# Four intermediate arrays of the first token block kept in the recurrence's on-chip buffers

## The chip, the cores and the metric

The kernel runs on one core of one Trainium2 chip. The metric is the device time of one execution in microseconds (us), lowest possible. All tensors are float32; the large matrix products split each operand into a rounded high part and a low rest, and take three matmuls for one product.

## The reference, cut to what matters

One inference step of a small trunk for 1024 prompt tokens and 8 x 16 sample tokens, width 1024, 16 heads of 64. Layer 0 is an RWKV-7 time mixing with a SwiGLU feed-forward part, layer 1 an attention in bands with another feed-forward part. The change lies in the time mixing of layer 0:

```python
r = xr @ w_r
w_log = -softplus(-(w0 + tanh(xw @ w1) @ w2)) - 0.5
decay = exp(-exp(w_log))
k = xk @ w_k
v = xv @ w_v
a_gate = sigmoid(a0 + (xa @ a1) @ a2)
g = sigmoid(xg @ g1) @ g2
kk = l2_normalize(heads(k * k_k))
k = k * (1.0 + (a_gate - 1.0) * k_a)
y, state = wkv7_scan(r, decay, k, v, -kk, kk * a_gate, state0)
...
bonus = sum_per_head(r * k * r_k) * v
out = ((groupnorm(y) + bonus) * g) @ w_o
```

Here `xr`, `xw`, ... are six mixes of each token's normed input with that of the token before it.

## The kernel before, in words

The 1152 tokens are three blocks b = 0, 1, 2 of 384 (`NB`, `TB`). For each block `proj(b)` computes the projections, feature tile by feature tile: f = 0 to 7, a tile being 128 features x 384 tokens. Its parts run in this order:

- `proj_lora`: the small products with w1, a1 and g1, then `second("w2", ..., "cs")` and `second("a2", ..., "a")`. For each f they put two matmuls into a PSUM bank of the tag `acc` (two banks), take a sigmoid on ScalarE (ACT, line 548) and, for the decay, a running sum along the tokens on VectorE (DVE, line 550). The results are the decay sums **cs** and the rates **a**. After that the gate g is evicted (line 596) and spilled.
- `proj_k`: for each f, 24 matmuls with `rw_k` into an `acc` bank. From cs two exponentials (lines 649 and 651), from a the factor of the key (line 658), from the bank a square (line 654), its sum over each head by one more matmul into the bank `aux`, a reciprocal root (lines 660 to 662) and six products on DVE (lines 663 to 674). Line 665 is the last that reads the bank. One result is the modified key **kp**. Three others are spilled to DRAM for the recurrence.
- `proj_r`: the same 24 matmuls with `rw_r`; with cs (line 514) and kp (line 515) it makes the scaled r and, by one more matmul, the **bonus** factor bn (line 521).
- `proj_v`: with `rw_v`; it multiplies v by bn (line 614).

The four arrays cs, a, kp and bn pass from one part to the next through DRAM: `save` (line 501) writes a tile of 192 KB to `sf`, `load` (line 498) brings it back. Per f that is four writes and five reads (cs is read by `proj_k` and again by `proj_r`), all issued by SyncE (SP).

Beside the projections runs the recurrence, in windows of 128 tokens, w = 0 to 8, each in two halves of the heads. `inverses(b)` inverts the small triangular matrices of the block's three windows beside `proj_r(b)` and the parts behind it: `win_first` multiplies (bank `G`), the result goes through DRAM (`ld`, `L`), a loop of 30 short DVE instructions solves it (lines 814 and 815), it goes through DRAM again (`Z`, `TT`), and `win_merge` joins the pieces by DVE transposes (`t`, line 835) and small matmuls (bank `st`). The windows of block b run beside `proj(b + 1)`; those of the last block run beside the output projection `outproj` of the blocks before. They load their inputs from DRAM into the buffers of the tags `XL`, `BKT`, `UV` and `YL`, three of each. In block 0 no window runs yet. Until the first windows these buffers serve only as landing place for a few weights of the adaLN modulation at the start (`self.early`).

A scheduler puts the instructions of each engine in order, guided by a timeline of its own; each engine then works through its list strictly in order and waits at an instruction whose input is not there. So the order on PE, DVE, ACT and SP can change at places that the source does not touch. DMAs of these parts are issued by SP, those of the inverses partly by ACT; both queues, too, work in order.

The lines before that the steps below touch: 473 (`spill`), 498 and 501, 514 to 521, 548 and 550, 583 (the load of the table set for logarithm and exponential), 614, 649 to 674.

Of the kernel before, what the change touches and what calls it, by code (L numbers as in the profile page):

```python
# [10 lines left out]
AF = mybir.ActivationFunctionType  # L11
# [6 lines left out]
TB = 384  # L18
KF = 8
KAPPA = float(np.exp(-0.5))  # L20
# [116 lines left out]
def mm(nc, out, lhsT, rhs, start, stop):  # L137
    return nc.tensor.matmul(out, lhsT, rhs, start=start, stop=stop)  # L138


class Trunk:
# [110 lines left out]
    def split(self, hi, lo, x):  # L252
        self.nc.scalar.activation(hi, x, AF.Copy)  # L253
        self.nc.vector.tensor_tensor(lo, x, hi, ALU.subtract)  # L254
# [220 lines left out]
    def proj(self, b):  # L475

        if b == 0:
            self.lw = {}
            ring = (f() for _ in range(2) for f in self.early)
            self.ada = self.ada_steps((0, 2, 1, 3), "acc", 2, lambda: next(ring))  # L480
            self.A0 = [self.cp.tile([128, 9], F32, name=f"A0_{f}") for f in range(8)]
            self.proj_h(0)
            self.x = self.hsplit()
            self.ada = self.ada_steps(range(4, 12))
        x, k = self.x, self.mixed(2, b)
        yield from self.proj_lora(b, *x)
        r = self.mixed(0, b)
        yield from self.proj_k(b, *k)
        v = self.mixed(3, b)
        yield from self.alternate(self.inverses(b), self.proj_r(b, *r))  # L490
        if b + 1 < NB:
            self.proj_h(b + 1)
        yield from self.proj_v(b, *v)
        if b + 1 < NB:
            self.x = self.hsplit()

    def load(self, t, n, b, f):
        self.nc.sync.dma_start(t, self.sf[b][n][:, f])

    def save(self, n, b, f, t):  # L500
        self.nc.sync.dma_start(self.sf[b][n][:, f], t)

    def proj_r(self, b, hi, lo):

        nc = self.nc
        for f in range(8):
            W = self.wunit(self.pp, self.a["rw_r"][f])
            pz = self.bank("acc", 2)
            self.gemm(pz[:, :TB], W, hi, lo)
            kp = self.ev("ag", 2)  # L510
            self.load(kp, "kp", b, f)
            ex = self.ev("rr", 2)
            self.load(ex, "cs", b, f)
            nc.scalar.activation(ex, ex, AF.Exp, scale=-KAPPA)
            nc.vector.scalar_tensor_tensor(kp, pz[:, :TB], self.P("rk", f), kp, ALU.mult, ALU.mult)
            nc.vector.tensor_tensor(ex, ex, pz[:, :TB], ALU.mult)
            self.spill("r", b, f, ex)
            aux = self.bank("aux", 1)
            mm(nc, aux[:, :TB], self.C("bo"), kp, True, True)
            bn = self.ev("e0", 3)  # L520
            nc.scalar.activation(bn, aux[:, :TB], AF.Copy)
            self.save("bn", b, f, bn)
            yield

    def proj_lora(self, b, hi, lo):

        nc, pp = self.nc, self.pp
        split = lambda ts: tuple([self.hgroups(t)[i] for t in ts] for i in range(2))
        (hc, hp), (lc, lp) = split(hi), split(lo)

        def first(n, rows):
            pw = self.bank("acc", 2)
            W = self.lora_in(n)
            for i, (h, l) in enumerate(((hc, lc), (hp, lp))):
                for k in range(8):
                    s = slice(k * rows, (k + 1) * rows)
                    self.mm3(pw[:rows, :TB], W[i][0][:, s], W[i][1][:, s], h[k], l[k], i + k == 0, i + k == 8)
            return pw

        def second(n, t, bias, spill):  # L540
            wh, wl = self.wunit(pp, self.a[n])
            for f in range(8):
                fs = slice(f * 128, (f + 1) * 128)
                pz = self.bank("acc", 2)
                mm(nc, pz[:, :TB], wh[:, fs], t, True, False)
                mm(nc, pz[:, :TB], wl[0:64, fs], t[0:64], False, True)
                sg = self.ev("e0", 3)
                ins = nc.scalar.activation(sg, pz[:, :TB], AF.Sigmoid, bias=self.P(bias, f))
                if spill == "cs":
                    nc.vector.tensor_tensor_scan(sg, rs, sg, 0.0, ALU.mult, ALU.add)  # L550
                self.save(spill, b, f, sg)
                if f % 4 == 3:
                    yield
            self.last_sg = ins

        pw = first("wa1", 128)
        yield
        tw, ta = self.ev("ag", 2, F32R), self.ev("ag", 2, F32R)
        th = self.ev("kp")
        nc.scalar.activation(th[:64], pw[:64, :TB], AF.Tanh)  # L560
        self.split(tw[0:64], tw[64:128], th[:64])
        th = self.ev("kp")
        nc.scalar.activation(th[:64], pw[64:128, :TB], AF.Copy)
        self.split(ta[0:64], ta[64:128], th[:64])
        pg = first("g1a", 128)
        yield
        th = self.ev("kp")
        h, l = self.ev("rr", 2, F32R), self.ev("rr", 2, F32R)
        nc.scalar.activation(th, pg[:, :TB], AF.Sigmoid)
        self.split(h, l, th)  # L570
        pg = first("g1b", 32)
        yield
        th = self.ev("kp")
        t = self.ev("vv", 2, F32R)
        nc.scalar.activation(th[:32], pg[:32, :TB], AF.Sigmoid)
        self.split(t[0:32], t[32:64], th[:32])
        nc.scalar.activation(t[64:96], th[:32], AF.Copy)
        rs = self.ev("rs", 1)
        nc.sync.dma_start(rs, self.a["rs"][b // 2])
        yield from second("w2", tw, "w0", "cs")  # L580
        yield from second("a2", ta, "a0", "a")
        with self.tc.issue_after(self.last_sg.ins):
            nc.scalar.preload_act_table_set("natural_log_exp_and_others")
        ah, al = self.wunit(pp, self.a["g2a"])
        raw = pp.tile([128, 1024], F32, tag="raw", name=self.nm("raw"), bufs=self.nraw)
        nc.sync.dma_start(raw[:96], self.a["g2b"])
        bh = pp.tile([128, 1024], F32R, tag="whi", name=self.nm("whi"), bufs=self.nhi)
        nc.scalar.activation(bh[:96], raw[:96], AF.Copy)
        nc.vector.tensor_tensor(bh[64:96], raw[64:96], bh[64:96], ALU.subtract)
        for f in range(8):  # L590
            fs = slice(f * 128, (f + 1) * 128)
            pz = self.bank("acc", 2)
            self.mm3(pz[:, :TB], ah[:, fs], al[:, fs], h, l, True, False)
            mm(nc, pz[:, :TB], bh[:96, fs], t[:96], False, True)
            g = self.ev("e0", 3)
            nc.scalar.activation(g, pz[:, :TB], AF.Copy)
            self.spill("g", b, f, g)
            if f % 4 == 3:
                yield

    def proj_v(self, b, hi, lo):

        nc = self.nc
        for f in range(8):
# [2 lines left out]
            self.gemm(pz[:, :TB], W, hi, lo)  # L607
            if b in (2,):
                self.step(1)
            vv = self.ev("vv", 2)  # L610
            self.load(vv, "bn", b, f)
            v = self.ev("e0", 3)
            nc.scalar.activation(v, pz[:, :TB], AF.Copy)
            nc.vector.tensor_tensor(vv, vv, pz[:, :TB], ALU.mult)
# [18 lines left out]
    def proj_k(self, b, hi, lo):  # L633

        nc = self.nc
        self.eend = self.eends[b]
        for f in range(8):
            W = self.wunit(self.pp, self.a["rw_k"][f])
            pz = self.bank("acc", 2)
            self.gemm(pz[:, :TB], W, hi, lo)  # L640
            iv = self.ev("rr", 2)
            self.load(iv, "cs", b, f)
            ag = self.ev("ag", 2)
            self.load(ag, "a", b, f)
            ext = self.pp.tile([128, 408], F32, tag="ext", name=self.nm("ext"), bufs=1)
            for s, sx, n, i in self.spans(b):
                ev = ext[:, sx].rearrange("p (g t) -> p g t", t=n + 1)
                nc.gpsimd.memset(ev[:, :, 0:1], 1.0)
                nc.scalar.activation(ev[:, :, 1:], iv[:, s].rearrange("p (g t) -> p g t", t=n), AF.Exp, scale=-KAPPA)
                nc.gpsimd.tensor_copy(self.eend[:, f, i:i + ev.shape[1]], ev[:, :, n])  # L650
            nc.scalar.activation(iv, iv, AF.Exp, scale=KAPPA)
            sq = self.ev("sq", self.nsq)
            kk = self.ev("kk")
            nc.scalar.activation(sq, pz[:, :TB], AF.Square, scale=self.P("kk", f))
            aux = self.bank("aux", 1)
            mm(nc, aux[:, :TB], self.C("bo"), sq, True, True)
            kp = self.ev("kp")
            nc.scalar.activation(kp, ag, AF.Identity, bias=self.oka[:, f:f + 1], scale=self.P("ka", f))
            inv = self.ev("inv", self.nsq)
            nc.vector.tensor_scalar(inv, aux[:, :TB], 1e-24, None, ALU.max)  # L660
# [1229 lines left out]
```

## Time and profile before

| | |
|---|---|
| median of 3 runs | 3863.73 us (3863.69 to 3864.73) |
| span of the profiled execution, first to last instruction | 3893.4 us |
| mean granted TensorE clock over that span | 0.927 |
| TensorE (PE) matmuls busy | 3557.4 us, 91% |
| DVE busy | 2281.8 us, 59% |
| ACT busy | 1578.1 us, 41% |
| moved by DMA | 551.91 MB |

The profile gives the span of one execution and no other time of it; this span is 29.7 us longer than the median of the runs that were timed without a profile. Block 0 covers, in this profile, about 88 us (first sigmoid of the decay) to 320 us (last tile of `proj_v`): `second` and the gate to 130 us, `proj_k` to 195, `proj_r` to 250, `proj_v` to 320. The four stages are named A, B, C and D below.

Rows of a wait view read "engine, what it writes, line <- what ended the wait: us in total, times, longest". Rows of a timeline read "start, duration, engine, line, operation, out<-in, shapes, count [idle before it <- what ended that]"; with a count above 1 they merge neighbours. A row of a stretch gives for each engine the busy us and the count of instructions, then the granted TensorE clock (PEclk, 1 is full), the share of time in which the DMA engines were busy, and GB/s.

### The profile page before, as it was taken

Reading aid. Unit: us, or ns where it says so; the run is one execution under the profiler, and the core shown is the slowest. Engines: PE = TensorE matmul, PEld = TensorE weight load, DVE = VectorE, ACT = ScalarE, POOL = GpSimd, SP = SyncE. Lnnn points to the kernel's source line nnn. Section 1 sums busy time; section 2 is a strip of 40 time slices with the busy share of each in tenths; the row PEclk is TensorE's granted clock in tenths of the full one; section 3 lists DMA queues with packets and bytes.
Section 4 is the critical chain, followed back from the end, with each engine's and each line's share of the span. In section 5 each row is a group of like instructions: output and inputs, shape, how many; then the busy total and the mean of one; then the engine's idle time right before and its main releaser. Section 6 shows DMA issues by size and latency. Waiting matters only on the chain.

```text
span 3893.4 us, 72370 instructions
## 1 busy us (share of the span) xinstructions
PE 3557.4 (91%) x28662; PEld 3135.3 (81%) x28662; DVE 2281.8 (59%) x4355; ACT 1578.1 (41%) x2987; POOL 571.8 (15%) x473
## 2 busy tenths in 40 slices
PE   6789988988889789999999899888889899999999
PEld 4677777777667689999888789777777789999998
DVE  4567566666435775555456842576675765454567
ACT  4554545554213443333411253465654533333310
POOL 0000000000000154454000100000000264454000
PEclk8887988789768989999999999999999899999999
DMA  5775776577646522222655213355464422222521
GB/s 195 223 223 150 202 231 164 143 225 201 179 127 191 177 92 74 76 73 76 235 202 203 83 53 101 108 158 156 147 192 155 138 74 76 74 74 94 169 82 72
DMA packets 429347, 551.91 MB, mean 142 GB/s; under 512 B 128432, under 2 KB 297520, under 8 KB 424528
## 3 DMA queue, kind: packets, MB, share of 16 engines
q1 hardware_dynamic: 374864, 528.41, 42.9%
q10 hardware_dynamic: 54144, 18.89, 2.2%
q8 instruction: 225, 3.69, 0.4%
q14 instruction: 114, 0.93, 0.1%
HBM read 413.03 MB, written 134.12 MB: 141 GB/s over the span
## 4 chain that ended last, share of the span: by engine, by line
PE 62%; DMA 7%; DVE 6%; ACT 3%; issue 2%; SPq 1%; POOL 0%; ACTq 0%; DVEq 0%; POOLq 0%
PE S L138 31%; PE PT L138 15%; PE acc L138 7%; PE st L138 2%; PE O L138 2%; DVE h L254 1%; PE PT L1716 1%; PE G L138 1%; PE Y L138 1%; PE aux L138 1%; ACT pts L1717 1%; DMA h<-qT 0%; DMA h<-in_wq 0%; DVE wlo L254 0%; DVE x L325 0%
## 5 line engine op out<-in xcount | busy, mean ns | idle before, releaser
L138 PE MATMUL S<-h,w 128*128 128x320 f32 (+1 forms) x4944 | 697.6, 300 | 19.8 <-DVE h L254 6.3
L138 PEld LDWEIGHTS S<-h,w 128*128 128x128 f32 x4944 | 674.6, 192 | 30.2 <-DVE h L254 12.5
L138 PE MATMUL acc<-mx,whi 128*128 128x384 f32 (+1 forms) x1824 | 526.1, 366 | 35.3 <-ACT mx L253 11.0
L138 PE MATMUL S<-h,wh 128*128 128x320 f32 (+1 forms) x2844 | 530.2, 338 | 13.3 <-DVE h L1086 7.7
L138 PEld LDWEIGHTS S<-h,wh 128*128 128x128 f32 x2844 | 456.7, 190 | 69.6 <-issue 13.0
L138 PEld LDWEIGHTS acc<-mx,whi 128*128 128x128 f32 (+1 forms) x1824 | 343.8, 196 | 72.4 <-ACT mx L253 13.1
L253 ACT ACTIVATE w<-rq 128x512 fp32r<-128x512 f32 x308 | 192.3, 629 | 517.0 <-PE S L138 199.0
L254 DVE TENSOR_TENSOR w<-rq,w 128x512 fp32r<-128x512 f32 x308 | 271.0, 883 | 198.9 <-ACT w L253 198.0
L138 PE MATMUL PT<-h,w 128*128 128x320 f32 (+1 forms) x2448 | 354.7, 300 | 8.2 <-DVE w L254 3.1
L138 PEld LDWEIGHTS PT<-h,w 128*128 128x128 f32 x2448 | 337.3, 192 | 11.8 <-DVE h L254 5.3
L138 PE MATMUL acc<-mx,wlo 128*128 128x384 f32 (+1 forms) x912 | 330.8, 363 | 7.1 <-DVE wlo L254 7.1
L138 PE MATMUL PT<-h,wh 128*128 128x320 f32 (+1 forms) x1428 | 286.7, 344 | 10.6 <-DVE wh L254 3.9
L1275 POOL TENSOR_TENSOR t<-t,t 128x576 f32<-128x576 f32 (+1 forms) x132 | 216.3, 1639 | 410.4 <-ACT t L1282 289.4
L138 PEld LDWEIGHTS PT<-h,wh 128*128 128x128 f32 x1428 | 233.6, 190 | 39.8 <-issue 6.5
L254 DVE TENSOR_TENSOR wlo<-raw,whi 128x1024 fp32r<-128x1024 f32 (+1 forms) x123 | 145.4, 1185 | 100.8 <-ACT whi L253 88.6
L138 PEld LDWEIGHTS acc<-mx,wlo 128*128 128x128 f32 (+1 forms) x912 | 178.7, 196 | 19.3 <-DVE wlo L254 9.1
L253 ACT ACTIVATE whi<-raw 128x1024 fp32r<-128x1024 f32 (+1 forms) x123 | 125.0, 1022 | 139.5 <-PE acc L138 93.4
L254 DVE TENSOR_TENSOR h<-h,h 128x1024 fp32r<-128x1024 f32 (+4 forms) x112 | 122.9, 1111 | 86.1 <-ACT h L253 70.9
L253 ACT ACTIVATE h<-h 128x1024 fp32r<-128x1024 f32 (+4 forms) x112 | 103.3, 935 | 166.4 <-DMA h<-sd 111.0
L253 ACT ACTIVATE wh<-rq 128x512 fp32r<-128x512 f32 x124 | 74.7, 626 | 225.7 <-PE S L138 142.7
L1275 DVE TENSOR_TENSOR t<-S,t 128x576 f32<-128x576 f32 (+1 forms) x116 | 86.4, 745 | 127.0 <-PE S L138 126.9
L1342 DVE TENSOR_TENSOR h<-h,S 128x640 f32<-128x640 f32 (+1 forms) x150 | 111.9, 750 | 78.4 <-PE S L138 78.2
(415 smaller groups left out, 5662.6 us busy)
## 6 DMA issues: line engine op xcount, KB each, us to landing
h<-in_wada SPq DMA_DIRECT2D x64, 512.0 KB, 6.1
rq<-in_wg SPq DMA_DIRECT2D x88, 256.0 KB, 2.6
rq<-in_wu SPq DMA_DIRECT2D x88, 256.0 KB, 2.6
rq<-in_wd SPq DMA_DIRECT2D x88, 256.0 KB, 3.1
raw<-in_wada SPq DMA_DIRECT2D x32, 512.0 KB, 4.4
kc<-in_ck SPq DMA_DIRECT2D x16, 1024.0 KB, 5.2
vc<-in_cv SPq DMA_DIRECT2D x16, 1024.0 KB, 6.1
sd<-t SPq DMA_DIRECT2D x88, 160.0 KB, 1.9
```

What stands on the lines that cost most here:

```text
L138: return nc.tensor.matmul(out, lhsT, rhs, start=start, stop=stop)
L253: self.nc.scalar.activation(hi, x, AF.Copy)
L254: self.nc.vector.tensor_tensor(lo, x, hi, ALU.subtract)
L1275: eng.tensor_tensor(out, x, y, ALU.add)
L1342: nc.vector.tensor_tensor(y, y, d, ALU.add)
L1716: nc.tensor.transpose(pt[:, j * 128:(j + 1) * 128], P[:, j * 128:(j + 1) * 128], self.C("ident"))
L1717: nc.scalar.activation(pts[:, 0:nk * 128], pt[:, 0:nk * 128], AF.Copy)
```

## The change

For block 0 alone, cs, a, kp and bn are no longer written to DRAM and read back. `keep_open`, called once at the start, takes three buffers each of `XL`, `BKT` and `UV` and cuts them into 24 tiles of 384 columns: cs gets the eight tiles of two `XL`, kp those of the third `XL` and two `BKT`, a those of the three `UV` and the third `BKT`. bn takes a's tiles again once a is used up. Each step of block 0 writes its result into such a tile, and the next works there. In `proj_k` the exponential of cs now goes to a tile of its own (`iv`), since cs is needed again in `proj_r`. Blocks 1 and 2 stay as they were. The buffers go back to the windows when the last tile in them has been used.

```diff
             self.ada = self.ada_steps(range(4, 12))
+            self.keep_open()
...
-    def load(self, t, n, b, f):
-        self.nc.sync.dma_start(t, self.sf[b][n][:, f])
+    def keep_open(self):
+
+        tile = lambda i: self.early[i]()
+        cut = lambda t: [t[:, j * TB:(j + 1) * TB] for j in range(t.shape[-1] // TB)]
+        xl = [tile(9 + i) for i in range(3)]
+        bkt = [tile(3 + i) for i in range(3)]
+        uv = [tile(6 + i) for i in range(3)]
+        group = lambda ts: [c for t in ts for c in cut(t)]
+        self.kept = {"cs": group(xl[:2]), "kp": group(xl[2:] + bkt[:2]), "a": group(uv + bkt[2:])}
+        self.kept["bn"] = self.kept["a"]
+
+    def place(self, tag, bufs, n, b, f):
+
+        return self.kept[n][f] if b == 0 else self.ev(tag, bufs)
+
+    def fetch(self, tag, n, b, f):
+        t = self.place(tag, 2, n, b, f)
+        if b:
+            self.nc.sync.dma_start(t, self.sf[b][n][:, f])
+        return t
 
     def save(self, n, b, f, t):
-        self.nc.sync.dma_start(self.sf[b][n][:, f], t)
+        if b:
+            self.nc.sync.dma_start(self.sf[b][n][:, f], t)
...
-            kp = self.ev("ag", 2)
-            self.load(kp, "kp", b, f)
-            ex = self.ev("rr", 2)
-            self.load(ex, "cs", b, f)
+            kp = self.fetch("ag", "kp", b, f)
+            ex = self.fetch("rr", "cs", b, f)
...
-            bn = self.ev("e0", 3)
+            bn = self.place("e0", 3, "bn", b, f)
...
-                sg = self.ev("e0", 3)
+                sg = self.place("e0", 3, spill, b, f)
...
-            vv = self.ev("vv", 2)
-            self.load(vv, "bn", b, f)
+            vv = self.fetch("vv", "bn", b, f)
...
-            iv = self.ev("rr", 2)
-            self.load(iv, "cs", b, f)
-            ag = self.ev("ag", 2)
-            self.load(ag, "a", b, f)
+            cs = self.fetch("rr", "cs", b, f)
+            iv = cs if b else self.ev("rr", 2)
+            ag = self.fetch("ag", "a", b, f)
...
-            nc.scalar.activation(iv, iv, AF.Exp, scale=KAPPA)
+            nc.scalar.activation(iv, cs, AF.Exp, scale=KAPPA)
...
-            kp = self.ev("kp")
+            kp = self.place("kp", 2, "kp", b, f)
```

On SP's list 72 DMA rows of block 0 are gone, nine for each f; 144 of the same kind remain for blocks 1 and 2. The order changes on the other engines too. Two places of it matter below.

The first is ACT in stage A, where the sigmoids of the decay stand (before: line 548 into `e`, which is the buffer `e0`; `mx` and `mr` are the mixes that ACT prepares in between).

```order
L253 ACTIVATE mx_393<-mr_395 128x384
L548 ACTIVATE e_122_667<-acc_664,par 128x384
L440 ACTIVATE mr_402<-hb,om 128x384
L548 ACTIVATE e_124_674<-acc_671,par 128x384
L440 ACTIVATE mr_409<-hb,om 128x384
L253 ACTIVATE mx_400<-mr_402 128x384
L548 ACTIVATE e_126_681<-acc_678,par 128x384
```

The same place in the changed kernel (the sigmoid's line is now 566, line 665 is the exponential of `proj_k` for f = 0):

```order
L253 ACTIVATE mx_402<-mr_404 128x384
L566 ACTIVATE XL_372<-acc_671,par 128x384
L440 ACTIVATE mr_411<-hb,om 128x384
L566 ACTIVATE XL_372<-acc_676,par 128x384
L665 ACT_TABLE_LOAD
L665 ACTIVATE ext_908<-XL_372 128x6x64
L440 ACTIVATE mr_418<-hb,om 128x384
L566 ACT_TABLE_LOAD
L566 ACTIVATE XL_372<-acc_681,par 128x384
```

An exponential of `proj_k` has moved in among the sigmoids, since its input is there at once, and with it come two loads of an activation table that stood nowhere before: 17 in the program instead of 15. Six of the eight key factors (line 658 before, 674 now) moved forward in the same way, in among the sigmoids of a; before, two stood there.

The second place is PE at the seam of `proj_r` and `proj_v`, where the merge of window 0 stands (`st<-t`). Before it comes at the end of the second unit of `proj_v` (`acc_2885`, f = 1; `acc_2839` is f = 0):

```order
L138 MATMUL acc_2885<-mx_1422,whi_2881 128x384
L138 MATMUL acc_2885<-mx_1423,whi_2881 128x384
L138 MATMUL acc_2885<-mx_1422,wlo_2882 128x384
L138 MATMUL st_1676<-t_354_1670,Aab_1464 32x16 x2
L138 MATMUL acc_2839<-mx_1429,whi_2835 128x384
L138 MATMUL acc_2885<-mx_1429,whi_2881 128x384
L138 MATMUL st_1676<-t_354_1670,Aab_1464 32x16 x30
L138 MATMUL st_1716<-t_357_1710,Aab_1488 32x16 x32
```

Now it comes before the second unit (`acc_2772`, f = 1; `acc_2728` is f = 0; `aux_2010<-BKT` is the bonus of the last tile of `proj_r`):

```order
L138 MATMUL acc_2728<-mx_1331,wlo_2725 128x384
L138 MATMUL acc_2728<-mx_1338,whi_2724 128x384
L138 MATMUL st_1595<-t_322_1589,Aab_1401 32x16
L138 MATMUL aux_2010<-BKT_376,cst 128x384
L138 MATMUL st_1595<-t_322_1589,Aab_1401 32x16
L138 MATMUL G_2041<-pa_2038 64x64 x15
L138 MATMUL st_1595<-t_322_1589,Aab_1401 32x16
L138 MATMUL G_2041<-pa_2038 64x64
L138 MATMUL acc_2772<-mx_1324,whi_2768 128x384
L138 MATMUL acc_2772<-mx_1325,whi_2768 128x384
L138 MATMUL st_1595<-t_322_1589,Aab_1401 32x16 x29
L138 MATMUL st_1635<-t_325_1629,Aab_1425 32x16 x32
```

Counted over the whole list, 29 fewer projection matmuls (those into `acc`) stand ahead of this merge than before. Further on the windows have moved as well: a state step of the fifth window stands 72 projection matmuls earlier, and the second half of the last windows 71 earlier, just behind the start of `outproj(0)` instead of well inside it.

More of the change, by code (lines that the diff above doesn't have):

```diff
@@ L648, in proj_k @@
                 nc.gpsimd.memset(ev[:, :, 0:1], 1.0)
-                nc.scalar.activation(ev[:, :, 1:], iv[:, s].rearrange("p (g t) -> p g t", t=n), AF.Exp, scale=-KAPPA)
+                nc.scalar.activation(ev[:, :, 1:], cs[:, s].rearrange("p (g t) -> p g t", t=n), AF.Exp, scale=-KAPPA)
                 nc.gpsimd.tensor_copy(self.eend[:, f, i:i + ev.shape[1]], ev[:, :, n])
-            nc.scalar.activation(iv, iv, AF.Exp, scale=KAPPA)
+            nc.scalar.activation(iv, cs, AF.Exp, scale=KAPPA)
             sq = self.ev("sq", self.nsq)
```

## The prediction

> **What bounds the kernel now.** I read the page first, then the span in stretches around block 0, then the waits of these stretches, last the timeline where a wait was large. On the page, the chain that ended last, and PE and its clock in 40 slices of 97 us:
>
> ```profile
> PE   6789988988889789999999899888889899999999
> ...
> PEclk8887988789768989999999999999999899999999
> ...
> PE 62%; DMA 7%; DVE 6%; ACT 3%; issue 2%; SPq 1%; POOL 0%; ACTq 0%; DVEq 0%; POOLq 0%
> ```
>
> PE carries the chain, and is 80 to 90% busy in most slices. An edit pays here only where PE waits for what it removes, or where PE runs at a lower clock because it waited. Block 0 is slices 1 to 3. Its four stages A to D, and two stretches that come up below:
>
> ```profile
> 88.00:130.00 42.00, 33.66 (x91) 21.21 (x91) 19.37 (x26) 27.47 (x50) 0.19 (x1) 0.63 0.60 187
> 130.00:195.00 65.00, 49.06 (x259) 43.17 (x258) 44.90 (x78) 36.33 (x67) 2.82 (x15) 0.92 0.79 233
> 195.00:250.00 55.00, 48.86 (x397) 41.96 (x399) 36.96 (x77) 24.26 (x42) 0.00 (x0) 0.94 0.93 287
> 250.00:320.00 70.00, 55.46 (x760) 50.41 (x749) 43.84 (x97) 39.60 (x77) 0.00 (x0) 0.80 0.62 171
> 91.00:121.50 30.50, 25.10 (x51) 14.50 (x52) 14.48 (x22) 19.67 (x36) 0.00 (x0) 0.51 0.59 194
> 165.50:172.30 6.80, 4.46 (x40) 4.34 (x41) 3.60 (x7) 2.23 (x6) 0.30 (x2) 0.50 1.03 280
> ```
>
> PE idles 8.3, 15.9, 6.1 and 14.5 us in A to D (length less PE busy), 45 us in all. That is the most that waits can give back; beyond it there is only the clock.
>
> **What goes from the queue.** Each of the removed DMAs is of this kind:
>
> ```profile
> rr<-sf_cs SPq DMA_DIRECT2D x48, 192.0 KB, 4.0
> ```
>
> 72 of 192 KB are 14.2 MB. The stages move 187 x 42 + 233 x 65 + 287 x 55 + 171 x 70 (GB/s by us) = 50.8 MB, so the change takes 28% of the bytes, and 4.0 us from issue to landing out of each of four hand-overs.
>
> **Stage A.** Here `save` only writes. What it holds up is the buffer `e`, three deep, so ACT waits for a write to end:
>
> ```profile
> ACT e L548 <- DMA sf_a<-e: 3.1, 1, 3.1
> ACT e L596 <- DMA sf_a<-e: 1.9, 1, 1.9
> ACT ext L649 <- DMA rr<-sf_cs: 1.9, 1, 1.9
> PE acc L138 <- ACT e L548: 5.1, 5, 2.4
> ```
>
> ```profile
> 107.29 0.69 PE L138 MATMUL acc<-ag,whi 128*128 128x384 f32 x1 [2.40 <-ACT e L548]
> 113.26 1.28 ACT L583 ACT_TABLE_LOAD   x1
> 114.64 0.71 ACT L658 ACTIVATE kp<-ag,oka,par 128x384 f32<-128x384 f32 x1
> ```
>
> These three ACT waits, 6.9 us, go. Against them stand two more table loads of 1.28 us among the sigmoids (2.6), and six key factors of 0.71 that move in (4.3). The sigmoids feed PE's two banks, so ACT's time there partly is PE's. I take 6.9 - 2.6 - 2.0 (half of the key factors; the rest lies in ACT's idle time) = **+2.3** us. Bounds: none of the waits ends earlier and all additions count, 6.9 lost; all of PE's idle time in A goes, 8.3 gained (5.1 of it are its waits for the sigmoid).
>
> The Trainium skill ("ScalarE: Activation LUTs", section "What ACT_TABLE_LOAD costs") gives a switch of the set about 1.28 us for the load and 1.38 for a drain. The row has the same 1.28, but the next ACT instruction starts 0.1 us behind it; by the page, two switches would cost 2.8 us more and the sum would be about 3856.
>
> **Stage B.** Here the loads of a and cs end late:
>
> ```profile
> PE aux L138 <- ACT sq L654: 7.4, 4, 3.8
> PE acc L138 <- DVE kk L665: 6.0, 4, 2.4
> ACT kp L658 <- DMA ag<-sf_a: 8.5, 4, 4.2
> ```
>
> ```profile
> 142.05 0.51 PE L138 MATMUL acc<-mx,whi 128*128 128x384 f32 x2
> 142.40 0.34 PE L138 MATMUL acc<-mx,wlo 128*128 128x384 f32 x1
> 142.57 0.51 PE L138 MATMUL acc<-mx,whi 128*128 128x384 f32 x2
> 152.66 0.71 ACT L658 ACTIVATE kp<-ag,oka,par 128x384 f32<-128x384 f32 x1 [4.20 <-DMA ag<-sf_a]
> 155.48 0.62 PE L138 MATMUL acc<-mx,whi 128*128 128x384 f32 x2 [1.84 <-DVE kk L665]
> 160.29 0.71 ACT L658 ACTIVATE kp<-ag,oka,par 128x384 f32<-128x384 f32 x1 [3.28 <-DMA ag<-sf_a]
> 164.36 0.91 PE L138 MATMUL aux<-sq,cst 128*128 128x384 f32 x2 [3.77 <-ACT sq L654]
> 185.29 0.61 PE L138 MATMUL acc<-mx,whi 128*128 128x384 f32 x2 [2.38 <-DVE kk L665]
> ```
>
> ACT stands 4.20 us for a tile of a, and because it works in order the square of the next tile is late too; DVE's line 665 then frees the bank late, and PE waits 1.84. The same happens at 160 with 3.28 on ACT and 3.77 on PE. Both PE waits go. Of the 2.38 at 185 I count half, 1.2. Together **+6.8**. Bounds: what only follows the longest DMA wait, 3.8, and all waits of both kinds, 7.4 + 6.0 = 13.4.
>
> **The clock.** Behind the 3.77 wait the granted clock is 0.50 from 165.5 to 172.3; PE is busy 4.46 us of that. Without the wait I expect full clock, half the busy time: **+2.2**. The bounds are 0 (the clock falls anyway) and half of A's 25.10 at 0.51, +12.5.
>
> The Trainium skill ("TensorE: Matmul & The Clock Gate", section "The HAM clock gate (the "warmup" mystery)") lets the clock fall after an idle window of about 3.4 us and rise after as much busy time. The 3.77 wait agrees with it. In stage A the clock stays at 0.51 although the longest wait there for a sigmoid is 2.40, so no single row there shows which wait would have to go.
>
> **Stages C and D.** The waits behind loads of cs, kp and bn:
>
> ```profile
> ACT rr L514 <- DMA rr<-sf_cs: 5.0, 3, 3.2
> PE aux L138 <- DVE ag L515: 1.6, 1, 1.6
> ```
>
> ```profile
> DVE vv L614 <- DMA vv<-sf_bn: 3.6, 1, 3.6
> PE acc L138 <- DVE vv L614: 2.1, 3, 0.9
> ```
>
> ACT's 5.0 us are long, but little of it comes through to PE: 1.6 us for line 515 in C (I take **+1.3**, as the product must still follow the last matmul), and of the 2.1 for line 614 in D the longest one, **+0.9**. Upper bounds: all of PE's idle time in C, 6.1, and the 3.6 that DVE waits in D; lower, 0. The loads of the windows' `XL` now wait on SP until the spill from the first kept tiles has landed, about 4.0 us by the row of such a DMA. Behind it on SP stand weights of `proj_v`, which are not needed before 250, and inputs of `inverses`; I take nothing for it and let 3 us into the range.
>
> **What is late next.** If PE is earlier in B and C, the solver of `inverses` is what it meets:
>
> ```profile
> 200.09 1.97 PE L138 MATMUL G<-pa 64*64 64x64 f32 x32 [1.12 <-DMA pa<-sp_b]
> ...
> 244.82 0.90 DVE L835 STREAM_TRANSPOSE t<-TT 32x256 f32<-32x256 f32 x2 [1.44 <-DMA TT<-Z]
> 246.78 0.24 PE L138 MATMUL st<-t,Aab 16*32 16x16 f32 x4
> ```
>
> From the second `G` of window 0 to its merge pass 44.7 us: 30 short DVE steps and two trips through DRAM. They don't shrink with PE's waits, and the last trip ends just in time (DVE waits 1.44 us for `TT`). The merge now stands 29 `acc` matmuls earlier. One takes 0.175 us at full clock (three from 142.05 to 142.57), so PE is there 5.1 us earlier, and 3 more by the waits gone from C, so it could stand up to 8 us. The trips run while the DMA engines are 93% busy, and have 28% fewer bytes beside them, so I take less than half: **-3**, bounds -8 and 0.
>
> Sum: 2.3 + 6.8 + 2.2 + 1.3 + 0.9 - 3 = 10.5 us, all within block 0; what comes after it moves forward unchanged. That is made against the profiled span of 3893.4, which is 29.7 above the median of the runs; a difference of 10 us carries over as it is. 3863.7 - 10.5 = **3853**.
>
> **The rivals.** *The clock comes back in stage A too.* The 6.9 us of ACT waits are what spreads PE's work in A; without them PE may stay busy enough. It gives another 12.5 less the 2.2 counted, about 3843. For it speaks that half clock covers nearly the whole of A, against it that PE has 8.3 us of idle time there of which the table loads keep a part.
>
> *The gain is given back inside block 0.* The solver takes 8 instead of 3, and the sigmoid stage gains nothing: 10.5 - 5 - 2.3 = 3.2, so 3860.5. The 1.44 us of DVE's wait for `TT` speak for it; the lighter queue speaks against it.
>
> *Slower: the windows lose their cover.* The order puts a state step of the fifth window 72 `acc` matmuls earlier, and the second half of the last windows 71 earlier. If the window's inputs are not there, PE stands for it: 72 and 71 by 0.175 us are 12.6 and 12.4, 25 us. That windows do wait is seen between 900 and 1260:
>
> ```profile
> PE G L138 <- DMA BK<-sp_k: 12.2, 4, 6.3
> ```
>
> All of it gives 3853 + 25 = 3878; from 18 us uncovered it is slower than before. Against it: matmuls taken from the front stand behind it and fill later waits, and half of the windows are ready long before.
>
> *The change doesn't do what it says:* 3864. The order already shows the 72 rows gone.
>
> **How the numbers follow.** Forecast 0.43, with its own range of 3846 to 3859 (B at its lower bound and the solver at 6; or B higher by 4 and the solver at 0); the clock in A 0.18; given back 0.21; windows 0.16; not done 0.02. A measurement of this kernel can tell 0.2%, 7.7 us, from no change: faster is below 3856.0, slower above 3871.5. Faster: 0.40 of the forecast and 0.18, 0.58. Within: 0.03 of the forecast, 0.21 and 0.02, 0.26. Slower 0.16. The range reaches down past the clock rival with stage B larger, 3836, and up past the one given back, with 7 us of the windows' loss, 3868; outside lie most of the windows' chance and little else.
>
> **What would show it.** In the changed profile the waits of ACT for `sf_a` and `sf_cs` in the first 250 us are gone, B's PE busy share rises from 49 of 65, and DMA shares fall by about a quarter. A is right if the gate starts about 2 us earlier in spite of two table loads among the sigmoids. The clock is right if no half clock stands at `proj_k`'s third tile. The solver term is PE's wait at the first `st<-t`. The forecast is wrong if block 0 ends less than 3 us earlier or over 18 earlier, or if PE waits more for `st`, `G` or `S` behind 320 than before.

## The result, and the profile after

The changed kernel is **slower by 0.5%**: ratio 1.0050, 95% interval 1.0039 to 1.0061, from 20 runs of each (medians 3893.68 and 3870.57 us; their quotient, 1.0060, lies inside the interval). The prediction said 3853, faster, with 0.16 for slower.

The three runs that gave the time before are the three shortest of these 20, which spread from 3863.7 to 3885.6 us, and the profiled execution that the prediction read was a long one (span 3893.4). So the comparison below does not use it, but a second profile of the kernel before, taken beside the experiments (run `before_again`, span 3875.8), called the **control** here. The first rows are the control's, the second the changed kernel's; each slice is 97 us:

```profile
span 3875.8 us, 72370 instructions
PE   6788998988889799999999899789889799999999
PEclk9788898789789889999999999899999899999999
```

```profile
span 3891.1 us, 72206 instructions
PE   6889989988888789999999899799888799999999
PEclk8897999788679889999999999899999899999999
```

Counted from 1, the changed kernel has the better clock by a tenth in slices 2, 3, 5 and 7; it is worse by a tenth in slices 1 and 4, and in the three neighbours 10 to 12 (870 to 1160 us). First block 0, in the four stages of the prediction. The stages are cut at the same projection matmuls in both profiles; columns as before. The control:

```profile
87.60:128.40 40.80, 33.37 (x91) 21.83 (x92) 18.93 (x26) 26.78 (x48) 0.19 (x1) 0.62 0.64 198
128.40:194.00 65.60, 50.30 (x258) 44.17 (x258) 45.07 (x78) 36.21 (x68) 2.49 (x15) 0.87 0.76 228
194.00:255.00 61.00, 51.53 (x556) 45.00 (x554) 37.78 (x80) 24.64 (x44) 0.00 (x0) 0.87 0.91 281
255.00:320.90 65.90, 56.78 (x588) 51.74 (x582) 42.98 (x95) 39.01 (x77) 0.00 (x0) 0.76 0.61 161
```

The changed kernel:

```profile
86.00:127.50 41.50, 32.00 (x91) 20.71 (x92) 19.45 (x26) 33.24 (x58) 0.19 (x1) 0.67 0.34 106
127.50:187.40 59.90, 50.52 (x258) 45.60 (x257) 46.07 (x80) 36.58 (x69) 3.73 (x15) 0.89 0.61 173
187.40:247.50 60.10, 53.40 (x572) 46.02 (x571) 38.86 (x84) 21.52 (x38) 0.00 (x0) 0.89 0.70 203
247.50:305.00 57.50, 50.31 (x630) 44.64 (x629) 40.74 (x89) 38.99 (x75) 0.00 (x0) 0.91 0.62 163
```

The stages take 41.5, 59.9, 60.1 and 57.5 us, where the control takes 40.8, 65.6, 61.0 and 65.9: **14.3 us less** in block 0. The DMA engines are far less busy in A to C. No wait for `sf_a`, `sf_cs`, `sf_kp` or `sf_bn` is left in block 0. PE's two largest waits in stage B, first the control, then the changed kernel:

```profile
PE aux L138 <- ACT sq L654: 7.2, 4, 3.4
PE acc L138 <- DVE kk L665: 6.0, 4, 2.8
```

```profile
PE aux L138 <- ACT sq L670: 5.0, 3, 3.4
PE acc L138 <- DVE kk L681: 4.4, 4, 1.4
```

So the total shrinks, but the longest wait for a square (`sq`), 3.4 us, is still there. In the control it stands at 162 us; in the changed kernel it stands in the last pair of tiles, where ACT waits for a spill and works through its list ahead of the square:

```profile
169.90 0.52 ACT L667 ACTIVATE rr<-XL 128x384 f32<-128x384 f32 x1 [1.38 <-DMA sp_k<-rr]
173.93 0.56 ACT L670 ACTIVATE sq<-acc,par 128x384 f32<-128x384 f32 x1
174.54 0.91 PE L138 MATMUL aux<-sq,cst 128*128 128x384 f32 x2 [3.39 <-ACT sq L670]
```

So the gain in block 0 is there, and the loss lies behind it. To find where, I sum PE's busy time multiplied by the granted clock ("work done") in each profile, and compare the times at which equal work is done. The time to reach some work is the work itself, PE's idle time, and half of PE's busy time at half clock (the records of these profiles know two granted clocks, 1 and 0.5); the last two columns give the last two parts. Against the control the changed kernel stands like this:

| work done (us at full clock) | control at | changed kernel | of it idle | of it half clock |
|---|---|---|---|---|
| 200 | 313 | -13.7 | -9.1 | -4.6 |
| 400 | 566 | -14.0 | -7.1 | -6.9 |
| 650 | 891 | -12.5 | -10.9 | -1.6 |
| 850 | 1183 | +7.1 | -2.0 | +9.1 |
| 1000 | 1388 | -4.3 | -3.5 | -0.8 |
| 1200 | 1591 | +4.9 | -0.9 | +5.8 |
| 3300 | 3852 | +12.0 | +0.4 | +11.6 |

It keeps its lead to about 890 us and loses 20 us in the 300 behind it. In this pair of profiles 11 us of that come back by 1388 us, nearly all of it as half clock, and 9 are lost again by 1591; so one pair doesn't give the size of the loss, and the experiments below have to. In the stretch from 890 to 1190 the last six half windows of the recurrence run, with the last tiles of `proj_v(2)`, the rest of the adaLN steps and the start of `outproj(0)` beside them. The whole stretch from work 650 to work 1000, control and changed kernel:

```profile
890.60:1388.50 497.90, 419.33 (x4299) 340.24 (x4299) 280.99 (x601) 182.79 (x352) 41.85 (x37) 0.83 0.59 172
```

```profile
878.10:1384.20 506.10, 420.12 (x4299) 337.50 (x4297) 272.42 (x600) 180.76 (x345) 34.09 (x27) 0.83 0.58 172
```

PE idles 86.0 us there instead of 78.6. No single wait makes the difference. Some of PE's waits from the start of that stretch to about 1200 us, those that are large or have changed, the control's first:

```profile
PE G L138 <- DMA BK<-sp_k: 10.9, 4, 4.9
PE aux L138 <- DMA raw<-in_wada: 9.5, 6, 2.5
PE aux L138 <- DVE ag L515: 1.5, 1, 1.5
PE st L138 <- DVE y L1000: 1.0, 1, 1.0
```

```profile
PE aux L138 <- DMA raw<-in_wada: 11.3, 7, 3.1
PE G L138 <- DMA UV<-sp_v: 6.6, 1, 6.6
PE G L138 <- DMA BK<-sp_k: 4.1, 2, 3.6
PE aux L138 <- DVE ag L533: 4.1, 1, 4.1
PE st L138 <- ACT y L1007: 3.3, 2, 1.9
```

What PE waits for has changed with the windows' places: less for `BK`, more for `UV`, `ag` and `y`.

### The profile page after: what moved, and what is told of

It is laid out like the page before. It is cut to its first block, busy times and chain, and to the rows that moved or that the text cites. A ratio compares the mean times of both kernels' runs of the same rounds, so it can differ in the third digit from the quotient of the medians.

```text
span 3891.1 us, 72206 instructions
## 1 busy us (share of the span) xinstructions
PE 3557.4 (91%) x28662; PEld 3130.6 (80%) x28662; DVE 2279.7 (59%) x4355; ACT 1583.6 (41%) x2989; POOL 578.7 (15%) x473
## 4 chain that ended last, share of the span: by engine, by line
PE 70%; DMA 11%; DVE 9%; ACT 6%; issue 3%; SPq 1%; ACTq 0%; POOL 0%; DVEq 0%; POOLq 0%
PE S L138 31%; PE PT L138 15%; PE acc L138 12%; PE st L138 3%; PE O L138 2%; PE G L138 2%; DVE h L254 1%; PE Y L138 1%; PE PT L1732 1%; DMA mr<-yg 1%; PE aux L138 1%; DVE wlo L254 1%; ACT whi L253 1%; DMA vf<-in_wo 1%; DMA yg<-y 1%
## 5 line engine op out<-in xcount | busy, mean ns | idle before, releaser
L138 PE MATMUL S<-h,wh 128*128 128x320 f32 (+1 forms) x2844 | 530.5, 338 | 14.3 <-DVE h L1102 7.8
L254 DVE TENSOR_TENSOR h<-h,h 128x1024 fp32r<-128x1024 f32 (+4 forms) x112 | 122.7, 1110 | 78.6 <-ACT h L253 61.9
```

## The experiments

All ratios are against the kernel before, run beside the experiment on the same chip, with 95% intervals; 0.001 is 3.9 us. The theories are numbered in the expectations.

### The kernel before again, and the table loads

`before_again` has no edit.

> The kernel before, unchanged, for a profile that belongs to these times: the one that the prediction read has a span of 3893.4 us, longer than any of the 20 timed runs of that kernel (3863.7 to 3885.6). Every theory expects a ratio of 1.00 and a span near 3870. They differ in where this profile is ahead of the changed kernel's. Theory 1, the order (the changed kernel pays behind block 0 for windows that stand earlier on TensorE): after the end of block 0 (about 320 us) the changed kernel is 5 to 15 us ahead, and it loses 25 to 35 us between 320 and 1360. Theory 2, the table loads: it is behind by 5 us or more at 130 us already and keeps that. Theory 3, the buffers that are held longer: it loses between 250 and 400, where the first windows load.

Measured: ratio 1.0002 (0.9986 to 1.0019). Theory 2 fails at 130 us (the changed kernel is 0.9 us ahead there). Theory 3 fails in the form given: nothing is lost between 250 and 400, and the gain holds to 890. Theory 1 had the sign, but put 25 to 35 us of loss between 320 and 1360; the profiles show 20, all behind 890.

`late_exp` takes the exponentials out from among the sigmoids. On ACT that leaves 15 table loads, on PE the list is the changed kernel's, row for row:

```diff
-                nc.scalar.activation(ev[:, :, 1:], cs[:, s].rearrange("p (g t) -> p g t", t=n), AF.Exp, scale=-KAPPA)
+                with self.tc.issue_after(self.last_sg.ins):
+                    nc.scalar.activation(ev[:, :, 1:], cs[:, s].rearrange("p (g t) -> p g t", t=n), AF.Exp, scale=-KAPPA)
```

> The changed kernel with the first exponentials of the key stage held behind the last sigmoid of the rates; 15 table loads instead of 17, the order on TensorE as in the changed kernel. Theory 1 (order of the windows) and theory 3 (held buffers): still about 20 us slower than before, 3890, at most 3 us better than the changed kernel. Theory 2 (the table loads and what they delay): the loss is gone, 3870 or less.

Measured: ratio 1.0048 (1.0030 to 1.0066), as the changed kernel. The table loads don't make the loss.

### TensorE's list alone

A list can be fixed from outside the scheduler: each instruction of an engine gets an order-only edge to the one ahead of it in a given list.

```diff
+def queue_in(tc, engine, kinds, text):
+    ins = [i for i in tc.nc.cur_bb.bb.instructions if i.engine == engine and type(i).__name__ in kinds]
+    d = np.frombuffer(zlib.decompress(base64.b85decode(text)), dtype="<i2").astype(int)
+    o = np.cumsum(d + 1) - 1
+    info = mybir.DependencyInfo(mybir.DependencyClass.NoSync, mybir.DependencyReason.DATA)
+    for a, b in zip(o, o[1:]):
+        tc.add_manual_dep(ins[b], ins[a].name, info, reason="queue_in")
...
         Trunk(tc, a, o).build()
+        queue_in(tc, mybir.EngineType.PE, ('InstMatmult',), _Q_PE)
```

`_Q_PE` is the list, as positions in the order of the source. Four kernels: the changed one with PE's list of before (`pe_as_before`), the one before with PE's list of the changed kernel, and the changed one with before's list only behind or only ahead of 890 us.

> The changed kernel, but TensorE's whole list is held in the order of the kernel before; the other engines are ordered by the scheduler around it. Theory 1 (the new order on TensorE costs what block 0 gains and more): the loss is gone and block 0's gain of 13 to 17 us shows in the end, 3855 to 3862, ratio 0.995 to 0.998. Theory 3 (buffers held longer, which the order has no part in): as slow as the changed kernel, about 3893. Theory 4 (the order of the other engines or of the DMA queue makes the loss): between the two, nearer 3885.

> The kernel before, with all its DMAs, but TensorE's whole list in the order of the changed kernel. Theory 1: slower than before without any of the change's edits, by the 20 us of the changed kernel plus the 13 to 17 us that block 0 now doesn't gain: 3893 to 3910. Theory 3: as fast as before, 3873. Theory 4: 3873 to 3883.

> The changed kernel; TensorE's list keeps the changed order up to the end of block 2's value stage (about 890 us) and follows the kernel before from there. The profiles show 13 to 17 us of gain kept up to 890 and 20 lost between 890 and 1190. If the order of the last windows makes that loss: 3858 to 3866. If it is made by what the head hands over to them (which windows are ready, which buffers are free): 3885 to 3893.

> The other half: TensorE as before up to about 890 us, from there in the changed order. If the order of the last windows makes the loss: about 3890. If the head makes it: 3858 to 3866.

Measured: 1.0056 (1.0037 to 1.0075), 1.0096 (1.0068 to 1.0125), 1.0044 (1.0022 to 1.0066) and 1.0087 (1.0056 to 1.0117). Theory 1 in the form "PE's list alone" falls: with before's list on PE the loss stays. `pe_tail_as_before` lies near the branch that blamed what the head hands over, and `pe_head_as_before` outside both of its branches. But the second kernel is slower than before by 1% without any edit of the change, so an order alone can cost that much. In all four the lists of the other engines are ones that the scheduler made around a list that was not its own; three of the four ratios are above the changed kernel's 1.0050. The profile of `pe_as_before` does not even gain in block 0: it is 5.1 us behind the control at work 200. Whether the order makes the loss can't be told from one engine's list.

### All five lists, and two harmless swaps

`all_as_before` is the changed kernel with the lists of PE, DVE, ACT, GpSimd and SP all held in the order of before, without the 72 DMAs (and with the first nine loads of `XL` and two early copies into `UV` left free). `rest_as_before` does so only from 320 us on:

```diff
+        queue_in(tc, mybir.EngineType.PE, ('InstMatmult',), _Q_PE)
+        queue_in(tc, mybir.EngineType.DVE, (...), _Q_DVE)
+        queue_in(tc, mybir.EngineType.Activation, ('InstActivation', 'InstDMACopy'), _Q_ACTIVATION)
+        queue_in(tc, mybir.EngineType.Pool, (...), _Q_POOL)
+        queue_in(tc, mybir.EngineType.SP, ('InstDMACopy',), _Q_SP)
```

`swap_k` is the kernel before, where block 0 issues two loads in the other order, and `kk_first` the kernel before, where block 0 issues one product ahead of another:

```diff
-            iv = self.ev("rr", 2)
-            self.load(iv, "cs", b, f)
+            if b:
+                iv = self.ev("rr", 2)
+                self.load(iv, "cs", b, f)
             ag = self.ev("ag", 2)
             self.load(ag, "a", b, f)
+            if not b:
+                iv = self.ev("rr", 2)
+                self.load(iv, "cs", b, f)
```

```diff
-            nc.vector.tensor_tensor(kp, kp, pz[:, :TB], ALU.mult)
-            self.save("kp", b, f, kp)
+            if b:
+                nc.vector.tensor_tensor(kp, kp, pz[:, :TB], ALU.mult)
+                self.save("kp", b, f, kp)
             nc.vector.scalar_tensor_tensor(kk, pz[:, :TB], self.P("kk", f), inv, ALU.mult, ALU.mult)
+            if not b:
+                nc.vector.tensor_tensor(kp, kp, pz[:, :TB], ALU.mult)
+                self.save("kp", b, f, kp)
```

> The changed kernel with block 0 in its own order; from the end of block 0 on (about 320 us) all five lists (TensorE, VectorE, ScalarE, GpSimd, SyncE) are held in the order of the kernel before. Theory 1b (the reshuffled order behind block 0, of all engines together, makes the whole loss; the edits themselves gain in block 0): 13 to 17 us faster than before, 3858 to 3862, ratio 0.996. Theory 3 (the edits cost something later by themselves, whatever the order: buffers held, bytes moved at other times): 3885 to 3895, ratio 1.003 to 1.005.

> The changed kernel with all five lists in the order of the kernel before from the start, apart from the 72 DMAs that are gone, nine loads and two copies of the first windows, which must wait for the kept buffers. Theory 1b: no loss behind block 0, and in block 0 the waits for the removed DMAs gone, at least half of the 13 to 17 us: 3858 to 3868. Theory 3: 3885 or more. If the gain in block 0 needs the new order there: 3873.

> The kernel before, with no buffer kept and no DMA removed; only, in the key stage of block 0, the load of a is issued ahead of the load of cs. That alone makes the scheduler put all lists in another order from there to the end of layer 0. Theory 1b, in the form that any reshuffle costs (the order of the kernel before is a lucky one): 10 to 25 us slower than before, ratio 1.003 to 1.006. If only the changed kernel's order is bad: 3873, ratio 1.000.

> As the last, with another harmless swap: in the key stage of block 0 the product that gives kk is issued ahead of the one that gives the modified key, and nothing else is changed. Any reshuffle costs: 10 to 25 us slower, ratio 1.003 to 1.006. Only the changed kernel's order is bad: ratio 1.000.

| kernel | ratio | interval |
|---|---|---|
| `all_as_before` | 0.9968 | 0.9948 to 0.9989 |
| `rest_as_before` | 0.9986 | 0.9970 to 1.0003 |
| `swap_k` | 1.0064 | 1.0042 to 1.0085 |
| `kk_first` | 1.0022 | 1.0003 to 1.0042 |

This decides it. With all lists as before, the change is **faster** by 0.3%, 12 us, where with its own lists it is slower by 0.5%. No run holds the kernel before in its own lists, so what the holding costs by itself isn't measured; the traces have as many matmuls (28662) and DVE instructions (4355) with it as without. Block 0 of `all_as_before`, stage by stage, is 217.6 us long, 15.7 less than the control's 233.3:

```profile
90.10:128.40 38.30, 33.16 (x90) 21.23 (x91) 18.95 (x26) 26.49 (x48) 0.64 (x1) 0.64 0.38 116
128.40:185.20 56.80, 47.10 (x259) 41.44 (x258) 44.97 (x79) 36.83 (x70) 4.33 (x15) 0.97 0.63 181
185.20:238.40 53.20, 47.60 (x554) 40.66 (x553) 37.23 (x80) 23.07 (x42) 0.00 (x0) 0.97 0.76 223
238.40:307.70 69.30, 56.42 (x593) 51.95 (x582) 42.97 (x95) 39.69 (x79) 0.00 (x0) 0.80 0.55 144
```

and its stretch from work 650 to 1000 is as long as the control's:

```profile
877.60:1374.90 497.30, 419.76 (x4296) 339.00 (x4295) 281.59 (x600) 182.19 (x351) 44.13 (x39) 0.83 0.59 171
```

Theory 3, that the held buffers or the moved bytes cost later, falls. `rest_as_before` came out between its two branches (0.996 and 1.003 to 1.005). And `swap_k` loses more than the changed kernel without keeping a buffer or removing a DMA: by its profile, too, it is 7.3 us ahead at work 650 and 9.6 behind at 850. Its last half window stands early as well, at the start of `outproj(0)`, like the changed kernel's; `kk_first`, whose windows hardly move on PE behind 890 us, loses nothing in that stretch (-4.4 at 650, -6.2 at 850). Its ratio is under the 1.003 to 1.006 that "any reshuffle costs" expected, and its interval nearly reaches 1.

### Which part of the order

`hold_last` is the changed kernel with that one last half window put back on PE beside `outproj(0)`, by order-only edges from 15 matmuls of that projection; else its PE list differs from the changed one only around that place.

```diff
+    for big, spans in _HOLD:
+        for a, b in spans:
+            for k in range(a, b):
+                tc.add_manual_dep(ins[k], ins[big].name, info, reason="hold")
```

The other three put all five lists together from two pieces, cut at 890 us, with `queue_in` as above.

> The changed kernel with one constraint on TensorE: the small products of the very last half window (sample tokens, second half of the heads) stand where the kernel before has them, beside the first 210 matmuls of the first output projection, and not ahead of it. All else is ordered by the scheduler, nearly as in the changed kernel. Theory 6 (the loss is made by the place of this half window: 71 big matmuls that covered it now come later, alone): the 20 us lost between 890 and 1190 shrink to 5 or less, 3860 to 3875, ratio 0.996 to 1.000. If the place of this one half window is not the cause: as the changed kernel, 3890 to 3896, ratio 1.004 to 1.005.

> The changed kernel; up to 890 us in its own order, from there all five lists in the order of the kernel before. If the order behind 890 makes the loss: 13 us faster than before, 3860 to 3868, ratio 0.996 to 0.998. If the order ahead of 890 makes it too: 3880 or more.

> The changed kernel; up to 890 us all five lists in the order of the kernel before, from there in the changed kernel's own. If the order behind 890 makes the loss: the gain of 12 us of the run with all lists as before is lost again, 3880 to 3890, ratio 1.001 to 1.004. If the order ahead of 890 makes it: 3863 to 3868, ratio 0.997.

> The kernel before with none of the change's edits; up to 890 us in its own order, from there all five lists in the changed kernel's. If the order behind 890 costs by itself: about 20 us slower than before, 3895 to 3900, ratio 1.005. If not: ratio 1.000.

`hold_last`: 1.0054 (1.0031 to 1.0077). Theory 6 falls: the place of the last half window is not the cause, though it is the most visible sign of the changed order. Its stretch is still 515 us long. The others, in one table with those above ("before" and "changed" are the orders of all five lists):

| run | edits | block 0 | 320 to 890 | from 890 | ratio | interval |
|---|---|---|---|---|---|---|
| `all_as_before` | yes | before | before | before | 0.9968 | 0.9948 to 0.9989 |
| `rest_as_before` | yes | changed | before | before | 0.9986 | 0.9970 to 1.0003 |
| `tail_all_as_before` | yes | changed | changed | before | 1.0009 | 0.9992 to 1.0027 |
| `head_all_as_before` | yes | before | before | changed | 1.0025 | 1.0007 to 1.0044 |
| the changed kernel | yes | changed | changed | changed | 1.0050 | 1.0039 to 1.0061 |
| `before_again` | no | before | before | before | 1.0002 | 0.9986 to 1.0019 |
| `before_tail_as_after` | no | before | before | changed | 1.0069 | 1.0042 to 1.0096 |

Read in pairs: the changed order behind 890 us costs 0.0041, 0.0057 and, without any edit, 0.0067: **16 to 26 us**. The edits themselves gain 0.0034 and 0.0044 in equal orders: **13 and 17 us**. The order ahead of 890 costs 0.0041 and 0.0025; of its two parts, 0.0018 and 0.0023, neither stands clear of the intervals. An estimate from the intervals, taken as independent, gives such a difference 0.002 to 0.003 either way, so the sizes are rough while the signs of the others stand. `tail_all_as_before` missed its first branch: the order ahead of 890 costs as well.

The profiles say the same of the stretch from work 650 to 1000, with all 16 of them. Eight have TensorE's list of before there, or one like it (`kk_first`): 495 to 504 us in six of them, 517 and 519 in two; mean 503. Eight have the changed kernel's (`hold_last` but for one half window) or `swap_k`'s: 506 to 542, mean 519. PE idles 73 to 82 us in the first group and 81 to 90 in the second. Of the 16 us between the means, 8 are idle time and 8 are half clock. From work 1000 to the end the two groups take 2491 and 2494 us, so little of the loss lies there.

What stays open: which place of the stretch behind 890 us is to blame (moving one half window back did not help, and no wait stands out), and where the cost of the order ahead of 890 comes out, since the profiles show no loss up to there. Added up from the means of the profiles, a lead of 14 us at work 650, 16 lost to work 1000 and 3 behind it leave the changed kernel 5 us behind (an estimate), where the interval of the runs says 15 to 24.

## Why the prediction was wrong, point by point

- **Block 0's sum was near, its terms less so.** Predicted were 10.5 us of gain; this profile shows 14.3 from the start to the end of block 0. The five profiles that have the changed kernel's order of matmuls in block 0 (its own, `late_exp`, `hold_last`, `rest_as_before`, `tail_all_as_before`) take 219 to 225 us for it, three with the kernel before's lists take 231 to 234: 10.6 between the means. That the sum fits is in part luck, since stage D gave 8.4 here instead of 0.9, and made up for A and B. D's gain is the clock's: 31.8 us of half clock stand there in the control and 10.2 here, and PE loses 13.5 and 4.7 us by them. About 4 of the 8.4 belong to this profile (D takes 57.5 us here, 61.2 to 61.8 in the other four). Why the clock is better there isn't shown; the merges have moved over D's border with C.
- **Stage B and the clock** together were to give 6.8 + 2.2 = 9.0 and gave 5.7. "Both PE waits go" was too much: the 3.4 us wait for a square moved to 174.5 us, behind ACT's own list. The half clock moved with it. In the control it stands from 160.8 us for 10.2 us, in the changed kernel from 175.8 for 6.8, right behind that wait. In all, B has 17.1 us of half clock in the control and 13.7 in the changed kernel; what PE loses by it is 5.5 and 6.3 us, so the clock's term came to nothing there.
- **Stage C and the solver.** C gave 0.9, against 1.3 less the solver's 3. PE does not wait at the first `st<-t`: from the second `G` to the first transpose of the merge pass 36.4 us instead of the control's 45.8, so the merge is ready when PE comes to it. The 2.4 us that PE waits in the merge stand at a later step (`st<-TT`), where the control waits 2.9.
- **Stage A** gave -0.7 instead of +2.3, inside the bounds. Without the two table loads (`late_exp`) A takes 40.3 us, 0.5 less than the control, and the end is no better; in the old order (`all_as_before`) it takes 38.3, 2.5 less. So, by these single profiles, the new order on ACT took A's gain. ACT at the first of the new loads:

```profile
89.79 1.28 ACT L665 ACT_TABLE_LOAD   x1
91.08 0.52 ACT L665 ACTIVATE ext<-XL 128x384 f32<-128x384 f32 x1
```

  The exponential starts 0.01 us behind the load. The Trainium skill ("ScalarE: Activation LUTs", section "What ACT_TABLE_LOAD costs") adds a drain of about 1.38 us to each switch; here no such gap stands behind the load.
- **With the lists held** as before, A and B gain 2.5 and 8.8 us in the one profile of `all_as_before`, close to the 2.3 and 9.0 that were predicted for the edits.
- **The step that failed** is "what comes after it moves forward unchanged". It was written though the order already showed windows moved by some 70 matmuls in two places behind block 0. The term for it was held in a rival, "the windows lose their cover", with 0.16 and its price of 25 us, and stood in the sum as 0. Measured, the order costs more than the edits gain: by the pairs above 16 to 26 us behind 890 alone.
- **The rival had the sign and the size, not the mechanism.** The state step that stands 72 matmuls earlier costs nothing that the profile shows (the lead is 14.0 us at 566 and 12.5 at 891). The end of the windows is where the time goes, but by the order of all lists there, not by the 71 matmuls of cover for the last half window: `hold_last` gives these back and gains nothing.
- **The reason against the rival**, that matmuls taken from the front fill later waits, is doubtful at the end: in the changed kernel's trace 1583 matmuls of the windows and the adaLN stand from 1020 to 1185 us, between the last projection matmul and `outproj(0)`, with no projection matmul among them to fill a wait. In the control they are 1523, so this alone does not explain the difference, and that it makes the loss is argued, not shown.
- **The base.** Three runs and one profile stood for the kernel before; 20 runs put it 7 us later, and the profile held a stretch of half clock around 1150 us that six of the eight profiles with that order don't have. The sign does not hang on it: even against 3863.7 the changed kernel is slower.

## What to carry to other kernels

Where a scheduler orders the lists, an edit has two prices: what it does at its place, and what the new order does elsewhere. Measure them apart: hold all lists in the old order (one engine's list isn't enough) to price the edit, and make a harmless swap to see what a new order alone costs. In a kernel that was measured and kept as it is, a new order may not be a neutral draw: both harmless swaps here were slower, by 0.2 and 0.6% (two draws, and the first is barely clear of its interval). An edit that gains 0.3% needed its order held to show it.

## What the runs showed of the hardware that was not expected

The same order can take two lengths in the stretch behind 1100 us. The control, the profile that the prediction read, and `tail_all_as_before`, which has before's order there, for equal work (800 to 850 in the count above):

```profile
1118.00:1183.00 65.00, 54.89 (x739) 38.82 (x740) 28.69 (x71) 14.99 (x28) 0.00 (x0) 0.89 0.57 178
```

```profile
1124.80:1205.40 80.60, 70.51 (x733) 51.34 (x732) 28.21 (x69) 14.38 (x26) 0.00 (x0) 0.72 0.47 147
```

```profile
1107.10:1193.70 86.60, 75.19 (x769) 52.30 (x766) 28.86 (x73) 16.20 (x30) 0.00 (x0) 0.68 0.48 144
```

PE is busy 70 or 75 us for what takes 55, at a granted clock of 0.72 or 0.68 instead of 0.89. So a single profile can be 16 to 22 us off in one stretch with this order. Over the 26 runs of the kernel before on one chip, times from 3861 to 3899 us go in part with the mean granted clock: about 2.3 us for 0.001 of it, with a correlation of -0.6.
